# Partial sums of weight tiles made by DMA in DRAM, and nine more groups of seven products

## The chip, the cores and the metric

One core of one Trainium2 chip runs the whole program. The metric is the device time of one execution in microseconds; the median of several executions is compared. TensorE is called PE in the profile, VectorE DVE, ScalarE ACT, GpSimd POOL and SyncE SP.

## The reference

One decoder layer on 256 tokens of width 2048, in float32:

```python
u = rmsnorm(h, norm_mix_pre)
z, xbc, dt_raw, q, k, v = split(u @ w_in)          # w_in: 2048 x 12320
xbc = silu(causal_depthwise_conv(xbc, conv_w, conv_b))
y_ssm = rmsnorm_grouped(ssd_chunked(...) * silu(z)) # Mamba-2 scan, 32 heads
y_att = dilated window attention of q, k, v         # 16 heads
h = h + rmsnorm(concat(y_ssm, y_att) @ w_out, norm_mix_post)          # w_out: 4096 x 2048
hdn = relu(rmsnorm(h, norm_mlp_pre) @ w_up)                           # w_up: 2048 x 8192
h = h + rmsnorm((hdn * hdn) @ w_down, norm_mlp_post)                  # w_down: 8192 x 2048
```

Nearly all of the work is the four weight matrices, 269 MB in float32, each multiplied once by 256 tokens.

## The kernel before

**Precision by splitting.** Every float32 factor is split into a rounded part hi and the rest lo, and a product is three matmuls: hi·hi, hi·lo and lo·hi (lines 262 to 264). A weight tile is 256 rows by 512 columns, laid out as 128 partitions x 2 x 512 (`raw`, 512 KB). `fetch` (line 144) loads it on SP's queue, ScalarE writes hi (line 139), VectorE lo = raw − hi (line 140). There are four `raw` buffers (`RAWS`) and five pairs of hi and lo (`BUFS`); a load waits until VectorE has read the last tenant of its buffer, and ScalarE waits until TensorE has used the hi buffer's last tenant. In some stages three more places for raw tiles lie in `uc`.

**Groups of seven.** `unit` (line 362) works two neighbouring column blocks of 512 at once, over all rows of K in steps of 256. For one such step there are, per column block, a 2 x 2 block of weights (two row tiles) and a 2 x 2 block of activations (two K tiles by two halves of the tokens). The plain way (`row_tiles`) takes eight products of three matmuls, 24. `seven` (line 311) does a Strassen-Winograd step instead: seven products, 21 matmuls. It needs four sums of activations, made once per set of activations and kept (`sums_of_acts`, line 293, in the places listed in `room["sums"]`), and four sums of weight tiles, made by VectorE each time. With a0, a1 and b0, b1 the two row tiles of the two column blocks, it makes e0 = a0 + b0, e1 = e0 + b1, t4 = e1 + a1 and, in place, b0 + b1, by four adds of 128x512 (`add_in_line`, line 223), and then splits a (two tiles), e (two), the b pair and t4 (one). `combine_new` and `combine_onto` bring the seven accumulators together at the unit's last group.

Which steps go by seven is written out: `V_SEVENS` (1, 3, 5, 6) for the V columns of w_in (two units of eight steps), lists in the calls of `unit` for w_out and w_down, and `UP_SEVENS` (2, 4, 5) for w_up. Of the eight w_up double blocks, the first is done in another way, so seven units by `unit` remain: three in the first half of the hidden width, four in the second. After each half its part of w_down follows: two units of 16 steps.

**Order.** The steps of `weights` and `seven` are given priority over the rest (`AHEAD`) and are kept in order among themselves by `in_line`. Side work, such as the turning of the last block's outputs, waits in a queue (`waiting`) and one piece of it is started after each step by `pump`. `mix_to_up` is an order written out by hand that covers the norm between w_out and w_up. Pool does a few small sums in the SSD part and the power −1/2 of the norms (lines 134, 885 and 1160); after the SSD part these are all that it does.

**Memory.** Pools are stacks: `cp` holds constants for the whole program, `mp` and `ap` the middle part, and `hp`, opened after `mid.close()`, the second part. `in_place_of_h` lends the room of `h` (`ha`, `hb`) to the sums of activations while h waits in DRAM (`h_d`).

Of the kernel before, what the change touches and what calls it, by code (L numbers as in the profile page):

```python
# [10 lines left out]
F32 = mybir.dt.float32  # L11
# [5 lines left out]
P = 128  # L17
# [22 lines left out]
KB = 2  # L40
MASKED = -1.0e30
# [10 lines left out]
UP_SEVENS = (2, 4, 5)  # L52
V_SEVENS = (1, 3, 5, 6)

# [20 lines left out]
def hymba_layer(ctx: ExitStack, tc: tile.TileContext, x, norm_mix_pre, w_in, conv_w, conv_b, dt_bias, a_log,  # L75
# [38 lines left out]
    cst = cp.tile([P, consts.shape[1]], F32, name="cst")  # L114
    ident = cst[:, 0:P]
    triu = cst[:, P:2 * P]
    two = cst[:, 2 * P:2 * P + 32]
    m0 = cst[:, 2 * P + 32:3 * P + 32]
    m1 = cst[:, 3 * P + 32:5 * P + 32]
# [23 lines left out]

    def fetch(src, k0, c0, step=KB, into=None):

        raw = wp.tile([P, KB, NB], F32, name="raw", bufs=RAWS) if into is None else into
        for j in range(0, KB, step):
            rs = slice((k0 + j) * P, (k0 + j + step) * P)
            nc.sync.dma_start(raw[:, j:j + step], src[rs, c0:c0 + NB].rearrange("(k p) n -> p k n", p=P))
        return raw  # L150
# [23 lines left out]
    def in_place_of_h(acts):  # L174

        a = hp.tile([P, 3 * KB, 2, S], F32R, name="ha")
        room["sums"] = [a[:, k] for k in range(3 * KB)]
        if acts is part:
            b = hp.tile([P, KB, 2, S], F32R, name="hb")
            room["sums"] += [b[:, k] for k in range(KB)]  # L180
            room["sums"] += [hp.tile([P, 2, S], F32R, name="wpost", bufs=2) for _ in range(2)]
        else:
            b = hp.tile([P, NT, NB], F32, name="hb")
            room["shared"] = [[b[:, t] for t in range(NT)],
                              [hp.tile([P, NB], F32, name="wpost", bufs=2) for _ in range(NT)]]
        room["raw"] = None
        room["acts"] = acts
        sums_of.clear()

    def fetch_next(src, k0, c0):  # L190

        if room["raw"] is None:
            return fetch(src, k0, c0)
        turn = room["turn"]
        room["turn"] += 1
        n = KB * (turn % (RAWS + (NK - SUMS) // KB - 1) - RAWS)
        return fetch(src, k0, c0, into=None if turn < 0 or n < 0 else room["raw"][:, n:n + KB])
# [25 lines left out]
    def add_in_line(dst, a, b):  # L223
        with in_line():
            line["dve"] = nc.vector.tensor_tensor(dst, a, b, op=ALU.add)  # L225
# [85 lines left out]
    def seven(src, ca, cb, k, acc, more, first, last):  # L311
# [4 lines left out]
        with tc.high_priority(offset=AHEAD):  # L316
            raw_a = fetch_next(src, k * KB, ca)
            raw_b = fetch_next(src, k * KB, cb)
            e, t4 = sum_tile(), tmp()
            add_in_line(e[:, 0], raw_a[:, 0], raw_b[:, 0])  # L320
            add_in_line(e[:, 1], e[:, 0], raw_b[:, 1])
# [3 lines left out]
            add_in_line(raw_b[:, 0], raw_b[:, 0], raw_b[:, 1])  # L325
# [33 lines left out]
    def order_of(ks, by_seven):  # L359
        return [(k, k in by_seven) for k in ks]  # L360
# [66 lines left out]
    cw = cp.tile([P, 4, 32], F32, name="cw")  # L427
    bias_b = cp.tile([P, 32], F32, name="bias_b")
    a_b = cp.tile([P, 32], F32, name="a_b")
    skip_b = cp.tile([P, 32], F32, name="skip_b")  # L430
# [19 lines left out]
    def load_parameters():  # L450
# [4 lines left out]
        nc.sync.dma_start(cst[:, P:], consts[:, P:])  # L455
# [77 lines left out]
    with tc.high_priority(offset=2 * AHEAD), tc.manual_schedule():  # L533
        nc.sync.dma_start(cst[:, 0:P], consts[:, 0:P])
# [21 lines left out]
    rbq = cp.tile([P, S], F32, name="rbq")  # L556

    mid = ExitStack()
# [5 lines left out]
    dt = cp.tile([P, NT, 32], F32, name="dt")  # L564
    dA = cp.tile([P, NT, 32], F32, name="dA")
    acs = cp.tile([P, NT, 32], F32, name="acs")
    eacs = cp.tile([P, 32], F32, name="eacs")
    toend = cp.tile([P, 32], F32, name="toend")
# [250 lines left out]
    def two_values(vb):  # L819
# [16 lines left out]
        unit(w_in[:, COL_V:], vb, order_of(range(7), V_SEVENS), (7,), acc, more,  # L836
# [15 lines left out]
    waiting.append(in_place_of_last_heads())  # L852
    qk.append(keys_too(1))
# [225 lines left out]
    early = 5  # L1079
    for k in range(early):  # L1080
# [16 lines left out]

    new_h()
# [19 lines left out]
    unit(w_out, 0, order_of(range(early, 14), (6, 9, 12)), (14, 15), acc, more,  # L1118
# [25 lines left out]
    unit(w_out, 2, order_of((0, 6, 1, 9, 2, 12, 3, 4, 5, 8, 7, 10), (6, 9, 12, 4, 8, 10)), (11, 13, 14, 15), acc, more,  # L1144
# [91 lines left out]
    for hf in range(2):  # L1236
        if hf:
            in_place_of_h(act_u)
        for fb in range(0 if hf else 2, 8, 2):
            unit(w_up[:, hf * 4096:], fb, order_of(range(6), UP_SEVENS), (6, 7), acc, more,  # L1240
                 lambda x: combine_new(room["shared"], x), 0, (up_end(fb, 0), up_end(fb + 1, 1)))
            acc, more = more, acc
        if hf == 0:
            in_place_of_h(part)
            unit(w_down, 0, order_of(range(14), (4, 6, 9, 11, 13)), (14, 15), acc, more,
                 lambda x: combine_new(in_mw(0), x), 0, (onto(0), onto(1)))
            unit(w_down, 2, order_of((0, 1, 4, 2, 6, 3, 9, 5, 11, 7, 13, 8), (4, 6, 9, 11, 13)), (10, 12, 14, 15), more, acc,
# [17 lines left out]
    unit(w_down[4096:], 0, order_of(range(14), (3, 6, 8, 11, 13)), (14, 15), acc, more,  # L1265
# [4 lines left out]
    unit(w_down[4096:], 2, order_of((0, 1, 3, 2, 6, 4, 8, 5, 11, 7, 13, 9), (3, 6, 8, 11, 13, 9)), (10, 12, 14, 15), more, acc,  # L1270
# [24 lines left out]
```

## Time and profile before

| | |
|---|---|
| median of 3 runs | 1473.71 us (1473.21 to 1474.2) |
| profiled execution: first to last instruction (span) | 1471.1 us |
| what the median has beside that span | 2.6 us |
| PE, DVE, ACT, POOL busy | 1461.2, 1239.6, 861.1, 47.8 us |
| granted clock of TensorE | 0.998 |
| moved by DMA | 287.31 MB, 195 GB/s on average |

The program's runs are timed without the profiler; the profiled execution has no other time of its own than its span, so the two are set against each other by the 2.6 us. Busy time of an engine is the union of its instructions' rows, so rows that overlap (an instruction starts before the one ahead of it has ended) count once. In a table of stages each row is a stretch in us from the start, its length, then for each engine the busy us and the count of instructions, the granted clock, the share of time that the 16 DMA engines are busy on average, and the rate in GB/s. In a list of DMA issues the last number is the median from issue to landing.

### The profile page before, as it was taken

What the parts mean: (1) busy time and instruction counts of PE and PEld (TensorE: products, weight loads), DVE (VectorE), ACT (ScalarE), POOL (GpSimd) and SP (SyncE); (2) the same over time, 40 slices, a digit from 0 to 9 for tenths busy, and PEclk for the clock granted to TensorE, in tenths of its full rate; (3) what the DMA queues carried; (4) which work ended last, traced back from release to release, by engine and by line L of the source; (5) the groups of instructions that cost most, each with busy time, mean ns of one, the idle gap of its engine ahead of it and who ended that gap; (6) DMA issues with size and microseconds to landing.
All of it is one profiled execution on the core that took longest, in us unless ns stands there. A gap on an engine that the chain in (4) does not pass through costs nothing.

```text
span 1471.1 us, 20006 instructions
## 1 busy us (share of the span) xinstructions
PE 1461.2 (99%) x7216; PEld 1231.4 (84%) x7216; DVE 1239.6 (84%) x1849; ACT 861.1 (59%) x1188; POOL 47.8 (3%) x67
## 2 busy tenths in 40 slices
PE   9999999999999999999999999999999999999998
PEld 8888888888888888888888888888888888888886
DVE  6798797898497696588989989889887898989998
ACT  7475675465456565555557566655554666665553
POOL 0003100210000000000000000000000000000000
PEclk9999999999999999999999999999999999999999
DMA  7665566555657476566657566655665666576853
GB/s 272 208 205 182 179 184 194 174 172 167 177 168 207 122 208 192 191 229 210 204 177 237 165 194 201 210 175 191 213 223 174 201 201 205 172 235 202 273 200 114
DMA packets 151299, 287.31 MB, mean 195 GB/s; under 512 B 11696, under 2 KB 14624, under 8 KB 151200
## 3 DMA queue, kind: packets, MB, share of 16 engines
q1 hardware_dynamic: 143472, 272.50, 58.9%
q10 hardware_dynamic: 7728, 13.54, 2.8%
q8 instruction: 56, 0.92, 0.3%
q14 instruction: 43, 0.35, 0.1%
HBM read 281.78 MB, written 4.23 MB: 194 GB/s over the span
## 4 chain that ended last, share of the span: by engine, by line
PE 94%; DVE 3%; issue 1%; ACT 1%; DMA 1%; POOL 0%; POOLq 0%; SPq 0%; ACTq 0%; DVEq 0%
PE acc L393 17%; PE acc L262 12%; PE acc L263 12%; PE acc L264 12%; PE acc L396 9%; PE acc L345 4%; PE acc L346 4%; PE acc L344 4%; PE ps L263 3%; PE ps L262 3%; PE ps L264 3%; PE ps L346 2%; PE ps L344 2%; PE ps L345 2%; DVE lo L140 1%
## 5 line engine op out<-in xcount | busy, mean ns | idle before, releaser
L139 ACT ACTIVATE hi<-raw 128x1024 fp32r<-128x1024 f32 (+1 forms) x477 | 499.0, 1053 | 387.9 <-PE acc L393 111.9
L140 DVE TENSOR_TENSOR lo<-raw,hi 128x1024 fp32r<-128x1024 f32 (+1 forms) x477 | 579.9, 1220 | 135.7 <-ACT hi L139 127.9
L393 PE MATMUL acc<-ua,hi 128*128 128x512 f32 x680 | 186.3, 402 | 0.0
L393 PEld LDWEIGHTS acc<-ua,hi 128*128 128x128 f32 x680 | 119.7, 189 | 18.7
L262 PE MATMUL acc<-hi,ua 128*128 128x512 f32 x280 | 112.0, 400 | 0.0
L396 PEld LDWEIGHTS acc<-ua,lo 128*128 128x128 f32 x680 | 99.8, 189 | 11.6
L264 PE MATMUL acc<-hi,ua 128*128 128x512 f32 x280 | 109.3, 391 | 0.0
L263 PE MATMUL acc<-lo,ua 128*128 128x512 f32 x280 | 109.3, 390 | 0.0
L396 PE MATMUL acc<-ua,lo 128*128 128x256 f32 x680 | 102.9, 281 | 0.0
L262 PE MATMUL acc<-hi,sh 128*128 128x512 f32 x224 | 88.7, 397 | 0.0
L264 PE MATMUL acc<-hi,sl 128*128 128x512 f32 x224 | 87.3, 390 | 0.0
L263 PE MATMUL acc<-lo,sh 128*128 128x512 f32 x224 | 87.3, 390 | 0.0
L139 ACT ACTIVATE hi<-e 128x1024 fp32r<-128x1024 f32 x51 | 54.1, 1062 | 55.5 <-DVE e L225 50.3
L393 PE MATMUL acc<-uc,hi 128*128 128x512 f32 x272 | 77.6, 398 | 0.0
L263 PE MATMUL acc<-lo,ah 128*128 128x512 f32 x168 | 65.5, 390 | 0.4 <-DVE lo L140 0.4
L264 PE MATMUL acc<-hi,al 128*128 128x512 f32 x168 | 65.4, 389 | 0.0
L262 PE MATMUL acc<-hi,ah 128*128 128x512 f32 x168 | 65.4, 389 | 0.0
L264 PEld LDWEIGHTS acc<-hi,ua 128*128 128x128 f32 x280 | 52.6, 188 | 11.6
L140 DVE TENSOR_TENSOR lo<-e,hi 128x1024 fp32r<-128x1024 f32 x51 | 62.0, 1216 | 0.0
L262 PEld LDWEIGHTS acc<-hi,ua 128*128 128x128 f32 x280 | 52.6, 188 | 10.4 <-ACT ua L141 0.3
L263 PEld LDWEIGHTS acc<-lo,ua 128*128 128x128 f32 x280 | 52.7, 188 | 10.0
L264 PE MATMUL acc<-hi,uc 128*128 128x512 f32 x144 | 56.0, 389 | 0.0
(475 smaller groups left out, 3060.9 us busy)
## 6 DMA issues: line engine op xcount, KB each, us to landing
raw<-in_w_in_dram SPq DMA_DIRECT2D x189, 512.0 KB, 3.6
raw<-in_w_up_dram SPq DMA_DIRECT2D x128, 512.0 KB, 3.9
raw<-in_w_down_dram SPq DMA_DIRECT2D x110, 512.0 KB, 4.7
raw<-in_w_out_dram SPq DMA_DIRECT2D x46, 512.0 KB, 4.2
uc<-in_w_out_dram SPq DMA_DIRECT2D x18, 512.0 KB, 4.5
uc<-in_w_down_dram SPq DMA_DIRECT2D x18, 512.0 KB, 5.1
bc<-acs_d ACTq DMA_DIRECT2D x8, 512.0 KB, 4.5
xs<-in_x_dram SPq DMA_DIRECT2D x8, 256.0 KB, 6.3
```

What stands on the lines that cost most here:

```text
L139: return (nc.scalar.activation(hi, src, AF.Copy), nc.vector.tensor_tensor(lo, src, hi.bitcast(F32), op=ALU.subtract))
L140: nc.vector.tensor_tensor(lo, src, hi.bitcast(F32), op=ALU.subtract))
L262: nc.tensor.matmul(dst, a_h[:, r, ts], hi[:, j], start=begin and j == 0, stop=False)
L263: nc.tensor.matmul(dst, a_h[:, r, ts], lo[:, j], start=False, stop=False)
L264: product[t] = nc.tensor.matmul(dst, a_l[:, r, ts], hi[:, j], start=False, stop=end and j == KB - 1)
L344: nc.tensor.matmul(dst, a_h, hi[:, j], start=own and first, stop=False)
L345: nc.tensor.matmul(dst, a_h, lo[:, j], start=False, stop=False)
L346: nc.tensor.matmul(dst, a_l, hi[:, j], start=False, stop=own and last)
L393: nc.tensor.matmul(acc[f], hi[:, j, f * P:(f + 1) * P], u(k0 + j), start=k0 + j == 0, stop=False, skip_group_check=True)
L396: nc.tensor.matmul(acc[f][:, 0], lo[:, j, f * P:(f + 1) * P], u(k0 + j)[:, 0], start=False, stop=k0 + j == NK - 1, skip_group_check=True)
```

## The change

- **Sums in DRAM.** For every group of seven, b0 + b1 is made by DMA: Pool's queue copies b0 (256 KB) from the weights to one of five places in DRAM, and then copies b1 onto it with an add. `plan` lists all groups in order ahead of time, and `next_pair` issues the two transfers for the next one on the list. Four are issued ahead, behind the last heads of the SSD part; each group then asks for the one four groups later. The first use of a place is preceded by a small transfer from `sh`, which makes Pool wait until the SSD part has written it.
- **The group.** The b tile is loaded in two issues of 256 KB: the sum b0 + b1 from its place into `raw_b[:, 0]`, and b1 from the weights. VectorE makes e1 = a0 + (b0 + b1), e0 = e1 − b1 and t4 = e1 + a1: three adds instead of four.
- **Constants.** What only the first half reads (`triu`, `two`, the masks, the convolution's weights, `dt` and its like) moves from `cp` to a pool `fp` that `mid.close()` closes; `ident` becomes a tile of its own. In that room `hp` gets `hc`, a place for one more set of sums of activations.
- **More groups.** `UP_SEVENS` becomes (1, 2, 4, 5), and in both units of the first w_down half step 2 joins (4, 6, 9, 11, 13). That is 68 groups instead of 59. The order of the steps in the second of these units changes with it.

```diff
+PAIRS_AHEAD = 4
-UP_SEVENS = (2, 4, 5)
+UP_SEVENS = (1, 2, 4, 5)
...
+    mid = ExitStack()
+    fp = mid.enter_context(tc.tile_pool(name="fp", bufs=1))
+    ident = cp.tile([P, P], F32, name="ident")
+    cst = fp.tile([P, consts.shape[1] - P], F32, name="cst")
...
-    def fetch(src, k0, c0, step=KB, into=None):
+    def fetch(src, k0, c0, step=KB, into=None, pair=None):
         raw = wp.tile([P, KB, NB], F32, name="raw", bufs=RAWS) if into is None else into
+        if pair is not None:
+            nc.sync.dma_start(raw[:, 0], pair)
+            nc.sync.dma_start(raw[:, 1], src[(k0 + 1) * P:(k0 + 2) * P, c0:c0 + NB])
+            return raw
...
-        room["sums"] = [a[:, k] for k in range(3 * KB)]
+        room["sums"] = [a[:, k] for k in range(3 * KB)] + [hc[:, k] for k in range(KB)]
...
+    def next_pair():
+
+        if not pairs:
+            return
+        src, ca, k = pairs.pop(0)
+        cb = slice(ca + NB, ca + 2 * NB)
+        d = places[len(paired) % len(places)]
+        if len(paired) < len(places):
+            nc.gpsimd.dma_start(d[:, 0:1], sh[:, NK - 1, 0:1].bitcast(F32))
+        nc.gpsimd.dma_start(d, src[k * KB * P:(k * KB + 1) * P, cb])
+        nc.gpsimd.dma_start(d, src[(k * KB + 1) * P:(k * KB + 2) * P, cb], accum_op=ALU.add)
+        paired.append((src, ca, k, d))
+
+    paired = []
+    places = [dram.tile([P, NB], F32, name=f"pair{i}") for i in range(PAIRS_AHEAD + 1)]
+
+    def pair_of(src, ca, k):
+
+        next_pair()
+        s_, c_, k_, d = paired[turn_of["pair"]]
+        assert (s_ is src) and (c_, k_) == (ca, k), (c_, k_, ca, k)
+        turn_of["pair"] += 1
+        return d
...
             raw_a = fetch_next(src, k * KB, ca)
-            raw_b = fetch_next(src, k * KB, cb)
+            raw_b = fetch_next(src, k * KB, cb, pair_of(src, ca, k))
             e, t4 = sum_tile(), tmp()
-            add_in_line(e[:, 0], raw_a[:, 0], raw_b[:, 0])
-            add_in_line(e[:, 1], e[:, 0], raw_b[:, 1])
+            add_in_line(e[:, 1], raw_a[:, 0], raw_b[:, 0])
+            add_in_line(e[:, 0], e[:, 1], raw_b[:, 1], ALU.subtract)
             hl_a = parts()
             split_in_line(*hl_a, raw_a)
             add_in_line(t4, e[:, 1], raw_a[:, 1])
-            add_in_line(raw_b[:, 0], raw_b[:, 0], raw_b[:, 1])
...
+            plan(("down", 0), w_down, 0, range(14), (2, 4, 6, 9, 11, 13))
+            plan(("down", 0), w_down, 2, (0, 2, 1, 4, 3, 6, 5, 9, 7, 11, 8, 13), (2, 4, 6, 9, 11, 13))
...
+    with tc.high_priority(offset=AHEAD):
+        for _ in range(PAIRS_AHEAD):
+            next_pair()
     qk.append(keys_too(1))
...
+    hc = hp.tile([P, KB, 2, S], F32R, name="hc")
+    hp.tile([P, S], F32, name="edge_h")
     new_h()
```

More of the change, by code (lines that the diff above doesn't have):

```diff
@@ L834, in end @@
             return at_end
-        unit(w_in[:, COL_V:], vb, order_of(range(7), V_SEVENS), (7,), acc, more,
+        unit(w_v, vb, orders["v", vb], (7,), acc, more,
              lambda x: combine_new([[v[:, t] for t in range(NT)] for v in values], x), 0, (end(0), end(1)))
@@ L1078, in hymba_layer @@
     acc = [bank() for _ in range(2 * NT)]
-    early = 5
-    for k in range(early):
+    for k in range(EARLY):
         for b in range(2):
@@ L1116, in whole @@
         return at_end
-    unit(w_out, 0, order_of(range(early, 14), (6, 9, 12)), (14, 15), acc, more,
+    unit(w_out, 0, orders["out", 0], (14, 15), acc, more,
          lambda x: combine_new(in_mw(0), x), 0, (whole(0), whole(1)), first=False)
@@ L1239, in hymba_layer @@
         for fb in range(0 if hf else 2, 8, 2):
-            unit(w_up[:, hf * 4096:], fb, order_of(range(6), UP_SEVENS), (6, 7), acc, more,
+            unit(w_ups[hf], fb, orders[("up", hf), fb], (6, 7), acc, more,
                  lambda x: combine_new(room["shared"], x), 0, (up_end(fb, 0), up_end(fb + 1, 1)))
```

77 lines of the change are left out of this document (46 added, 31 removed).

## The prediction

> **What bounds the kernel now.** I read the page's engine line and chain first, then the table of stages, then one group of seven instruction by instruction, and last the transfers.
>
> ```profile
> span 1471.1 us, 20006 instructions
> PE 1461.2 (99%) x7216; PEld 1231.4 (84%) x7216; DVE 1239.6 (84%) x1849; ACT 861.1 (59%) x1188; POOL 47.8 (3%) x67
> PE 94%; DVE 3%; issue 1%; ACT 1%; DMA 1%; POOL 0%; POOLq 0%; SPq 0%; ACTq 0%; DVEq 0%
> ```
>
> TensorE is busy over 99% of the span and carries 94% of the chain that ended last, so only fewer matmuls, or new holes between them, move the time. VectorE at 84% is second. That is an average; what matters is how close it comes to the length of each stage.
>
> ```profile
> core 0: us, PE busy (x) PEld busy (x) DVE busy (x) ACT busy (x) POOL busy (x), PEclk, DMA share, GB/s
> 409.00:449.00 40.00, 39.73 (x180) 32.65 (x179) 37.23 (x45) 23.37 (x27) 0.00 (x0) 1.00 0.66 195
> 628.00:689.00 61.00, 61.00 (x271) 50.53 (x271) 53.27 (x71) 33.22 (x40) 0.00 (x0) 1.00 0.71 237
> 866.00:909.70 43.70, 43.70 (x201) 36.11 (x200) 38.70 (x47) 28.40 (x36) 0.00 (x0) 1.00 0.64 196
> 952.70:1041.00 88.30, 88.30 (x396) 73.05 (x395) 77.78 (x102) 48.44 (x56) 0.00 (x0) 1.00 0.60 197
> 1041.00:1110.00 69.00, 69.00 (x306) 57.11 (x306) 60.02 (x70) 37.72 (x40) 0.00 (x0) 1.00 0.63 213
> 1295.10:1386.40 91.30, 91.30 (x410) 75.54 (x409) 86.25 (x114) 51.52 (x62) 0.00 (x0) 1.00 0.70 234
> 1386.40:1452.00 65.60, 65.19 (x288) 53.63 (x287) 61.61 (x76) 37.93 (x43) 0.00 (x0) 1.00 0.55 186
> ```
>
> In order: the first V unit, the end of the first W_out unit, one W_up unit (seven of these run), the two units of the first W_down half, the two of the second. Columns after the first are busy time with the count. A W_up unit leaves VectorE 43.70 − 38.70 = 5.0 us idle. Where VectorE fills 93 or 94% of the stretch TensorE loses a little: 0.27 us in the V unit, 0.41 us in the last one. At 94.5% (1295 to 1386, with fewer groups of seven per us) it loses nothing.
>
> **TensorE: 27 matmuls fewer.** A pair of K tiles for two column blocks costs 24 matmuls, as a group of seven 21. Groups now: V 8, W_out 9, W_up 7 × 3 = 21, W_down 21, together 59. After: W_up 7 × 4 = 28, first W_down half 12, the rest as before: 68. Nine more groups remove 27 matmuls of 128x512. The duration in a matmul's own row is about 390 ns, but they overlap, so the price is their spacing. Between 1041 and 1110 nearly all work is such matmuls and nothing is idle: 69.00 / 306 = 0.2255 us. 27 × 0.2255 = **6.1 us**, all on the bounding path: seven units lose 3 × 0.2255 = 0.68 us each, two more lose the same.
>
> **VectorE.** One group of seven, in order of time:
>
> ```profile
> start us, us, engine line op out<-in xcount [idle before <-releaser]
> 880.85 0.68 DVE L225 TENSOR_TENSOR e<-raw 128x512 f32<-128x512 f32 x1
> 881.57 0.69 DVE L225 TENSOR_TENSOR e<-e,raw 128x512 f32<-128x512 f32 x1
> 882.18 1.22 DVE L140 TENSOR_TENSOR lo<-raw,hi 128x1024 fp32r<-128x1024 f32 x1
> 883.31 0.69 DVE L225 TENSOR_TENSOR r<-e,raw 128x512 f32<-128x512 f32 x1
> 883.92 0.69 DVE L225 TENSOR_TENSOR raw<-raw 128x512 f32<-128x512 f32 x1
> 884.52 1.22 DVE L140 TENSOR_TENSOR lo<-e,hi 128x1024 fp32r<-128x1024 f32 x1
> 885.87 1.23 DVE L140 TENSOR_TENSOR lo<-raw,hi 128x1024 fp32r<-128x1024 f32 x1
> 887.01 0.68 DVE L140 TENSOR_TENSOR lo<-r,hi 128x512 fp32r<-128x512 f32 x1
> 887.61 0.68 DVE L225 TENSOR_TENSOR e<-raw 128x512 f32<-128x512 f32 x1
> ```
>
> Again the spacing is the cost. The `raw<-raw` add is the sum b0 + b1 that the change takes from DRAM instead: 884.52 − 883.92 = 0.60 us less in each of the 59 groups, 35 us over the kernel. The whole group takes 887.61 − 880.85 = 6.76 us, afterwards 6.16. A pair done the plain way has two 1024 splits of 883.31 − 882.18 = 1.13 us, 2.26. So a pair turned into a group adds 3.9 us of VectorE. A W_up unit goes from 38.70 to 38.70 − 3 × 0.60 + 3.9 = 40.8 us, while TensorE shrinks it to 43.70 − 0.68 = 43.0: 95% full, idle 2.2 us instead of 5.0. The first W_down half's first unit goes to 77.78 − 5 × 0.60 + 3.9 = 78.7 of 87.6, which still has room. V, W_out and the second W_down half only get lighter.
>
> One more set of activation sums is made three times (twice for W_up, once for W_down), each one add of 512, three smaller ones and a split:
>
> ```profile
> L302 DVE TENSOR_TENSOR r<-ah,al 128x512 f32<-128x512 f32 x11 | 7.5, 684 | 0.0
> L303 DVE TENSOR_TENSOR r<-r 128x256 f32<-128x256 f32 x23 | 9.7, 422 | 1.4 <-PE acc L1223 0.7 <-PE ps L1141 0.2
> L304 DVE TENSOR_TENSOR r<-r 128x128 f32<-128x128 f32 x23 | 6.7, 289 | 0.5
> L305 DVE TENSOR_TENSOR r<-r 128x128 f32<-128x128 f32 x23 | 6.6, 287 | 0.4
> ```
>
> That is 0.68 + 0.42 + 2 × 0.29 + 0.68 = 2.4 us at most, 7 us in all, beside TensorE; the W_down one lands in the unit above (81.1 of 87.6). I cost it at nothing; with the cover gone it is up to 7 us.
>
> I take what a VectorE that is 95% full costs TensorE from the two stretches at 93 and 94%: 0.3 us a unit, 7 × 0.3 = **2.1 us lost**. Those two stretches get 4 and 6 adds lighter, so their 0.27 and 0.41 us should go: **0.7 us gained**.
>
> **Transfers.** Per group the change adds on Pool's queue a copy of 256 KB from DRAM to DRAM and an accumulating copy of 256 KB onto it; the SP queue then reads that sum in place of b0, so what SP moves stays the same, in one more instruction (0.37 us, below). No run shows an accumulating transfer or one issued by Pool.
>
> ```profile
> q1 hardware_dynamic: 143472, 272.50, 58.9%
> 880.96 0.37 SPq L149 DMA_DIRECT2D raw<-in_w_up_dram  x1
> raw<-in_w_up_dram SPq DMA_DIRECT2D x16, 512.0 KB, 4.3
> q10 hardware_dynamic: 956, 2.86, 14.6%
> raw<-in_w_out_dram SPq DMA_DIRECT2D x16, 512.0 KB, 5.6
> raw<-in_w_down_dram SPq DMA_DIRECT2D x24, 512.0 KB, 4.9
> h_d<-ha ACTq DMA_DIRECT2D x6, 256.0 KB, 4.3
> ha<-h_d ACTq DMA_DIRECT2D x6, 256.0 KB, 6.9
> ```
>
> Row 1: 0.589 × 16 × 1471.1 / 143472 = 0.097 us per 2 KB packet. 256 KB is 128 rows, 8 packets on each of 16 engines, 0.77 us. I price the copy at 0.77 and the accumulate between 0.77 (one pass) and 1.54 (source and sum both read), and take 0.77, as every packet in the trace has that price. Four groups a W_up unit: 6.2 to 9.2 us of the 16 engines on top of 0.64 × 43.7 = 28, so the share rises from 0.64 to 0.79, or 0.87.
>
> What that does to the loads is read from stretches with a second queue at work. In the W_up unit a load lands 4.3 us after its issue; at share 0.71, beside the second queue's 14.6%, 5.6; at 0.70 in the second W_down half, 4.9. The two loaded stretches (61.00 of 61.00, 91.30 of 91.30) cost TensorE nothing. The slack: the load issued at 880.96 holds the second matrix of the group that VectorE starts at 887.61; landing at 885.3 it is 2.3 us early. After the change the group ahead is 0.60 shorter and the tile takes two issues (0.37), so 1.4 us are left: a landing up to 5.7 us is free. I expect 5 to 5.7 and charge nothing.
>
> The Trainium skill speaks against the change here: "Collectives: The Full Stack", section "The bandwidth ceiling: the fold count and why AG ≠ RS ≠ AR", says that an add made in the transfer reads two sources, and so runs at about half a copy's rate. By it the accumulate takes 1.54 us; no run here shows it yet.
>
> Pool waits for the copy before it issues the accumulate, and for the read of the place's last tenant. Behind these on Pool stand only the square roots of the later norms, issued after the last group ahead of them, and nobody needs them sooner. The moved constants are the same transfers into other tiles; I cost them at nothing, covered by the first weight tiles' work.
>
> **Sum.** −6.1 + 2.1 − 0.7 = −4.7 us on the profiled span, 1471.1 to 1466.4. The median of the runs, 1473.71, lies 2.6 us above that span and I keep this offset: **1469.0 us**. A measurement of this kernel can tell about 0.2%, 2.9 us, from no change; faster means below 1470.8, slower above 1476.7.
>
> **Rivals.**
>
> *Late loads (slower).* The place: the load of the b tile ahead of each of a W_up unit's four groups. A load that meets the copy and a doubled accumulate lands at 4.3 + 0.77 + 1.54 = 6.6 us instead of 4.3; starting from the 4.9 of W_down, 7.2. I price the middle, 6.9: 1.2 us past the free 5.7, four times a unit, 4.8, of which 2.2 idle VectorE time covers part: 2.6 × 7 = 18 us, less the 6.8 saved: **about 1485 us**. Milder, at 6.5, it is 1.0 × 7 = 7, no gain. It turns to a loss when landing passes 6.5 us. For it: the share of 0.87 is above anything in the trace. Against it: idle transfer time between bursts, and loaded stretches that cost nothing.
>
> *VectorE sets the W_up units (no change).* The units stay at 43.7 because 95% cannot be scheduled without holes; the gain is only W_down's 2 × 0.68 and the 0.7: 1473.7 − 2.1 = **1471.6 us**. For: 39.73 of 40.00 at 93%. Against: nothing lost at 94.5%.
>
> *The sums come late, so the change does not do what it says (slower).* SP would wait for a sum with all later loads behind it. A pair takes copy plus accumulate; by the last two rows 4.3 to 6.9 us each, 8.6 to 13.8. A W_up unit asks for one every 43.0 / 4 = 10.8 us, four ahead. At 13.8, with no overlap between pairs, a unit takes 55 us: 7 × 12 = 84 us more, **1551 us**. Against: the next copy can start while an accumulate is in flight.
>
> **How the numbers follow.** Forecast 0.56 (1466.9 to 1470.7: the holes between 0 and 0.55 us a unit), VectorE-bound 0.12, late loads 0.28, late sums 0.04. Faster 0.56, within 0.2% 0.12, slower 0.32. The range runs from 1466.4, no holes at all with the gaps gone (1473.7 − 6.8) less the 0.5 by which the runs shown differ from their median, to 1482, which takes in the milder two thirds of the late-load case; the rest and the late sums are left out. The forecast's own range is 1466.9 to 1470.7.
>
> **What would show it.** Matmuls 7189; 68 rows of three adds instead of 59 of four; VectorE near 40.8 us in a W_up unit, and its length 43.0 to 43.5 us. Landings of `w_up` loads at 5 to 5.7 us confirm the transfer step; above 6.5, with ScalarE or VectorE waiting for `raw` ahead of groups and holes between matmuls, the late-load rival holds. SP waiting on Pool's transfers would show late sums. The prediction is wrong if W_up units are longer than 43.7 us.

## The result, and the profile after

The changed kernel takes 1494.51 us (median; 1492.58 to 1496.69) against 1473.46 us for the kernel before on the same chip: ratio 1.0143, 95% interval 1.0131 to 1.0155. It is 21 us slower, where 4.7 us faster was forecast. The profiled execution, whose span is 1494.9 us, is the longest of the four, 2.2 us above their median. Its page, as far as it answers to the lines shown of before:

```profile
span 1494.9 us, 20376 instructions
PE 1466.0 (98%) x7189; PEld 1224.8 (82%) x7189; DVE 1240.7 (83%) x1850; ACT 871.4 (58%) x1209; POOL 143.5 (10%) x208
q1 hardware_dynamic: 144560, 272.50, 58.3%
q0 software_dynamic: 15392, 35.66, 11.9%
PE 64%; DVE 16%; DMA 12%; ACT 4%; issue 3%; POOL 0%; SPq 0%; POOLq 0%; DVEq 0%; ACTq 0%
```

The 27 matmuls are gone (7216 to 7189), and the engines' busy times have hardly moved. What moved is the chain: TensorE carried 94% of it and carries 64% now; VectorE has 16% and DMA, which had 1%, 12%. Pool's queue q0 is new, 11.9% of all sixteen engines' time. No single engine became the bound; the chain passes through transfers and VectorE's work instead.

`unit` works seven double blocks of w_up, W_up units 1 to 7. Here are 2, 3, 5, 6 and 7 (1 and 4 follow another stage), in the columns of the table of stages; the W_up row shown of before was unit 2, 43.70 us with all 43.70 busy, and the others were 43.0 to 44.3 us long:

```profile
871.80:916.40 44.60, 43.44 (x198) 35.22 (x197) 40.41 (x50) 29.21 (x39) 5.44 (x8) 1.00 0.82 231
916.40:964.10 47.70, 45.44 (x207) 36.51 (x206) 40.27 (x49) 30.15 (x40) 4.89 (x7) 1.00 0.79 229
1180.70:1225.50 44.80, 44.78 (x205) 36.74 (x204) 40.08 (x49) 29.24 (x38) 5.45 (x8) 1.00 0.84 236
1225.50:1273.30 47.80, 44.10 (x197) 34.86 (x197) 40.48 (x50) 29.68 (x39) 5.45 (x8) 1.00 0.81 225
1273.30:1320.70 47.40, 44.67 (x205) 35.97 (x204) 40.21 (x48) 30.15 (x39) 4.89 (x7) 1.00 0.80 226
```

VectorE has 40.1 to 40.5 us, near the forecast 40.8, and the DMA share is 0.79 to 0.84. Two units are nearly as long as before, three are 3 to 5 us longer, at the same share and the same work. So what costs the time is not in the sums of these columns; the traces below look for it in which instruction meets which transfer.

The loss by stage, worked out from the records: by how much the stage is longer than before, and behind L what TensorE lost there, the sum over neighbouring matmul starts of what they are apart beyond 0.227 us (counted from 0.06 us on). The last columns are kernels from the experiments below.

```
us            after         no transfers  acc. alone    acc. behind    order 0,3,1..
                            (a_src)       (a_acc)       small copy     (a_0312)
V1           +0.7  L 7.7   -2.1  L 6.1   -2.3  L 6.0   +0.0  L 6.2   -1.0  L 6.2
V2           +2.7  L 3.4   +0.9  L 2.2   +1.3  L 2.2   +0.4  L 3.2   +2.4  L 3.0
W_out        -0.5  L 2.6   +0.7  L 2.6   +0.3  L 2.6   +0.7  L 2.6   -0.4  L 2.6
W_up 1       +2.8  L 5.8   +2.0  L 5.3   +2.4  L 5.5   +2.5  L 5.5   +0.0  L 4.7
W_up 2-3     +5.7  L 5.3   +1.1  L 2.3   +1.3  L 2.8   +5.1  L 4.8   +3.7  L 1.1
W_down, up 4 +5.9  L10.6   +0.0  L 2.0   -0.5  L 2.1   +3.6  L 7.7   +3.5  L 8.8
W_up 5-7     +8.3  L 9.3   -2.3  L 1.9   +0.5  L 3.6   +4.8  L 6.7   +1.0  L 1.8
W_down 2     -2.8  L 0.4   -1.2  L 0.3   -1.6  L 0.3   -2.5  L 0.8   -2.9  L 0.4
the end      +1.0  L 3.2   +1.2  L 3.2   +1.0  L 3.2   +1.3  L 3.2   +1.1  L 3.2
all          L 48.2        L 25.9        L 28.2        L 40.6        L 31.8
```

The kernel before has L 21.0 in all; by stage, in the same order, 6.8, 2.2, 2.6, 2.7, 0.7, 0.8, 1.1, 1.0 and 3.2. (What the changed kernel loses more in V1 it loses in the first 108 us, ahead of Pool's first transfer.) The changed kernel lost 27 us more between its matmuls, which turned the 6 us of fewer matmuls into a loss. Two kinds of hole stand out; how the 27 us divide between them and others is not worked out.

**Late loads.** The chain of waits at the end of W_up unit 6, then Pool's and TensorE's instructions of the same moment:

```profile
1259.12 8.59 DMA raw<-in_w_up_dram
1267.70 0.02 issue
...
1267.81 1.06 ACT hi L143
1268.87 0.61 ACT junk L1270
1269.48 0.61 ACT r L1270
...
1270.52 0.62 ACT r L1271
```

```profile
1256.93 0.81 POOL L258 DMA_DIRECT2D pair<-in_w_down_dram  x1 [6.52 <-DMA pair<-in_w_down_dram]
1268.38 0.39 PE L311 MATMUL acc<-hi,uc 128*128 128x512 f32 x1
1270.66 0.55 PE L1282 MATMUL ps<-ident,junk 128*128 128x128 f32 x3 [1.90 <-ACT junk L1271]
```

Line 258 is the accumulate. It is issued at 1256.93 and, by its record, lands at 1265.73. Three loads of weights are issued behind it, at 1257.24, 1259.12 and 1261.45, and land at 1266.37, 1267.70 and 1268.97, one behind the other and all behind it: 7.5 to 9.1 us, where 4 are usual. ScalarE stands at the split of the first for 5.4 us, and behind that split in its queue wait the scalings of unit 6's own first outputs (`junk` and `r`, lines 1270 and 1271). TensorE needs those for its transposes and starts them 2.3 us after the last matmul. The engines' waits over the whole run point the same way; the first two lines are of the kernel before, the others of the changed one:

```profile
ACT hi L139 <- DMA raw<-in_w_up_dram: 23.9, 23, 1.6
ACT hi L139 <- DMA raw<-in_w_down_dram: 20.2, 17, 3.1
```

```profile
ACT hi L143 <- DMA raw<-in_w_up_dram: 37.7, 31, 5.4
ACT hi L143 <- DMA raw<-in_w_down_dram: 35.6, 26, 4.9
DVE e L233 <- DMA raw<-pair: 19.7, 14, 3.9
POOL pair L257 <- DMA raw<-pair: 542.1, 44, 74.6
```

(Us in total, times, longest.) The last line says that Pool mostly waits for a place to be read: the sums are not late. That an engine other than TensorE waits costs nothing in itself; the chain above shows one place where it did.

**A bank handed over.** The start of the same unit:

```profile
1230.82 1.22 DVE L144 TENSOR_TENSOR lo<-e,hi 128x1024 fp32r<-128x1024 f32 x1
...
1231.96 1.22 DVE L144 TENSOR_TENSOR lo<-raw,hi 128x1024 fp32r<-128x1024 f32 x1
...
1233.09 0.68 DVE L144 TENSOR_TENSOR lo<-r,hi 128x512 fp32r<-128x512 f32 x1
1233.69 1.28 DVE L144 TENSOR_TENSOR sl<-acc,sh 128x512 fp32r<-128x512 f32 x2
1234.43 0.19 PEld L390 LDWEIGHTS acc<-hi,ha 128*128 128x128 f32 x1 [2.04 <-DVE sl L144]
```

With step 1 a group of seven, the products of the unit's second step want the `acc` banks in which the last unit's outputs still stand, turned and waiting to be split (`sl<-acc`). These splits stand in VectorE's queue behind three splits of the group itself. TensorE's weight load waits 2.0 us for them, a wait that no row of before has: there step 1 was plain. Over the whole run TensorE idles 5.3 us for such splits, in four places:

```profile
PE acc L390 <- DVE sl L144: 2.7, 2, 1.6
PE acc L390 <- DVE al L144: 2.6, 2, 1.5
```

### The profile page after: what moved, and what is told of

Its sections match the earlier page's. It is cut to its first block, busy times and chain, and to the rows that moved or that the text cites. A ratio compares the mean times of both kernels' runs of the same rounds, so it can differ in the third digit from the quotient of the medians.

```text
span 1494.9 us, 20376 instructions
## 1 busy us (share of the span) xinstructions
PE 1466.0 (98%) x7189; PEld 1224.8 (82%) x7189; DVE 1240.7 (83%) x1850; ACT 871.4 (58%) x1209; POOL 143.5 (10%) x208
## 3 DMA queue, kind: packets, MB, share of 16 engines
q0 software_dynamic: 15392, 35.66, 11.9%
## 4 chain that ended last, share of the span: by engine, by line
PE 64%; DVE 16%; DMA 12%; ACT 4%; issue 3%; POOL 0%; SPq 0%; POOLq 0%; DVEq 0%; ACTq 0%
PE acc L449 17%; DVE lo L144 10%; PE acc L452 8%; PE acc L309 7%; PE acc L311 7%; PE acc L310 7%; DMA raw<-pair 4%; DMA raw<-in_w_down_dram 4%; DMA raw<-in_w_up_dram 3%; DVE e L233 3%; ACT hi L143 2%; PE acc L392 2%; PE acc L390 2%; PE acc L391 2%; PE ps L310 1%
## 5 line engine op out<-in xcount | busy, mean ns | idle before, releaser
L143 ACT ACTIVATE hi<-e 128x1024 fp32r<-128x1024 f32 x60 | 63.7, 1061 | 114.3 <-DVE e L233 105.8
L309 PE MATMUL acc<-hi,ua 128*128 128x512 f32 x236 | 94.0, 398 | 0.0
L310 PE MATMUL acc<-lo,ua 128*128 128x512 f32 x236 | 92.2, 391 | 0.0
L311 PE MATMUL acc<-hi,ua 128*128 128x512 f32 x236 | 92.1, 390 | 0.0
L309 PE MATMUL acc<-hi,sh 128*128 128x512 f32 x212 | 84.0, 397 | 0.0
L311 PE MATMUL acc<-hi,sl 128*128 128x512 f32 x212 | 82.6, 390 | 0.0
L310 PE MATMUL acc<-lo,sh 128*128 128x512 f32 x212 | 82.6, 390 | 0.0
L144 DVE TENSOR_TENSOR lo<-e,hi 128x1024 fp32r<-128x1024 f32 x60 | 73.1, 1218 | 0.0
L309 PE MATMUL acc<-hi,uc 128*128 128x512 f32 x144 | 56.0, 390 | 1.5 <-ACT hi L143 1.5
L233 DVE TENSOR_TENSOR e<-raw 128x512 f32<-128x512 f32 x55 | 37.8, 687 | 23.1 <-DMA raw<-pair 19.7
L310 PE MATMUL acc<-lo,uc 128*128 128x512 f32 x144 | 56.0, 389 | 0.0
L311 PE MATMUL acc<-hi,uc 128*128 128x512 f32 x144 | 56.0, 389 | 0.0
```

The source lines that it names most:

```text
L143: return (nc.scalar.activation(hi, src, AF.Copy), nc.vector.tensor_tensor(lo, src, hi.bitcast(F32), op=ALU.subtract))
L144: nc.vector.tensor_tensor(lo, src, hi.bitcast(F32), op=ALU.subtract))
L233: line["dve"] = nc.vector.tensor_tensor(dst, a, b, op=op)
L309: nc.tensor.matmul(dst, a_h[:, r, ts], hi[:, j], start=begin and j == 0, stop=False)
L310: nc.tensor.matmul(dst, a_h[:, r, ts], lo[:, j], start=False, stop=False)
L311: product[t] = nc.tensor.matmul(dst, a_l[:, r, ts], hi[:, j], start=False, stop=end and j == KB - 1)
```

## The experiments

Three theories stood at first. The bank handover (A in the expectations); the transfers, whose landings come late (the prediction's first rival); and a VectorE that is too full. Each kernel's time is set against runs of the kernel before on the same chip.

### Undoing one part

```diff
 a_src, in the kernel after: no transfers by Pool, b0 is loaded in place of the sum
-            nc.sync.dma_start(raw[:, 0], pair)
+            nc.sync.dma_start(raw[:, 0], src[k0 * P:(k0 + 1) * P, c0:c0 + NB])
 a_0312: another order of W_up's steps;  a_0312_src: both
-                plan(("up", hf), w_ups[hf], n, range(6), UP_SEVENS)
+                plan(("up", hf), w_ups[hf], n, (0, 3, 1, 2, 4, 5), UP_SEVENS)
 a_59, in the kernel after: the old 59 groups (UP_SEVENS (2, 4, 5), old W_down lists)
 b145, in the kernel before: UP_SEVENS = (1, 4, 5)
```

> The changed kernel without Pool's transfers: the place of b0 + b1 is loaded with b0 itself from the weights, in the same two issues (so the sums are left out and the output is not the layer's). Groups, order and VectorE's work are those of the changed kernel. A: the handover stays, 1480 to 1486. B: the loss goes, 1467 to 1470. C: 1494.5.

1473.15 us, ratio 0.9996 (0.9987 to 1.0005): all 21 us are back, as theory B has it, but not the gain that it expected on top.

> The changed kernel with W_up's steps in the order 0, 3, 1, 2, 4, 5: the same 68 groups and the same transfers, but the first group stands at the third place again and four stand in a row. A: 10 to 14 us of the loss comes back, 1480 to 1484. B: 1494.5 within 3, the transfers are the same. C: four in a row are worse for VectorE, 1494.5 or more.

1484.76 us, 1.0074 (1.0055 to 1.0093): 10 us are back, with all transfers and all groups in place, just short of what theory A expected.

> The changed kernel with W_up's steps in the order 0, 3, 1, 2, 4, 5 and without Pool's transfers (b0 itself loaded in the sum's place, so the sums are left out and the output is not the layer's). Handover and transfers as two separate causes: both gone, 1467 to 1469, the 6.1 us of matmuls earned. If four groups in a row fill VectorE even with three adds: 1473 or more.

1473.33 us, 1.0000 (0.9990 to 1.0009): with no transfers the order is worth nothing.

> The kernel before with one edit: W_up's three groups of seven stand at steps 1, 4, 5 instead of 2, 4, 5. Same matmuls, same VectorE work, no transfer by Pool. Theory A (bank handover: a unit's first group of seven writes into the four banks from which the last unit's outputs are still being turned; at step 1 it does so one step earlier): W_up units 1.5 to 2 us longer, seven of them, 1484 to 1488 us. Theory B (Pool's transfers make the loads land late): 1473.5 within 2. Theory C (VectorE is full): 1473.5 within 2.

1478.45 us, 1.0036 (1.0023 to 1.0049): a group on step 1 costs the kernel before 5 us, less than half of what theory A expected, and more than the other two did.

> The changed kernel with the 59 groups of before: sums in DRAM, three adds, but W_up at 2, 4, 5 and the first W_down half without step 2. A: 1471 to 1474, first group at the third place and VectorE lighter. B: nine pairs of transfers fewer of 68 and 6 us of matmuls more: 1485 to 1495. C: VectorE lighter than before, 1473 or less.

1475.36 us, 1.0013 (1.0004 to 1.0023): sums in DRAM for the old groups cost 2 us and gain none, though VectorE's busy time falls from 1239.6 to 1207.0 us. Theory B, which expected 1485 to 1495 from the transfers alone, missed.

What follows: the loss needs Pool's transfers, and added groups beside them; with the old groups the transfers cost 2 us, and without the transfers the new groups cost nothing. With no transfers the order of W_up's steps is worth nothing (a_src against a_0312_src), with all of them 10 us. That is more than the handover itself: TensorE's idle time for `sl` and `al` is 5.3 us in the changed kernel, 1.2 in a_src, 1.1 in b145 and none in a_0312. The order also moves the loads against the transfers, and no run parts the two. Even with neither in the way nine groups and 27 matmuls fewer bring nothing: the holes grow from 21.0 to 25.9 us in a_src, and eat 4.9 of the 6.1.

### Which of the two transfers

```diff
 a_copy: the accumulate left out;  a_2copy: a plain copy in its place
-        nc.gpsimd.dma_start(d, src[(k * KB + 1) * P:(k * KB + 2) * P, cb], accum_op=ALU.add)
 a_acc: the copy left out after the first five
-        nc.gpsimd.dma_start(d, src[k * KB * P:(k * KB + 1) * P, cb])
+        if len(paired) < len(places):
+            nc.gpsimd.dma_start(d, src[k * KB * P:(k * KB + 1) * P, cb])
 a_half: groups 2 and 5 of each W_up unit load b0 themselves
```

> The changed kernel with the accumulating transfer left out: Pool issues the copy of b0 alone (the sums are not made, the output is not the layer's). Leaving out all of Pool's transfers gave back 21.4 us. If an accumulate reads two sources and takes two thirds of the pair's time on the DMA engines: 1480. If both weigh the same: 1484. If the copy from DRAM to DRAM is the dearer: 1487 or more.

1475.93 us, 1.0010 (1.0000 to 1.0019).

> The changed kernel with the copy left out behind the first five: Pool issues the accumulate alone, onto what the place held (the sums are wrong, the output is not the layer's). Accumulate two thirds: 1487. Both the same: 1484. Copy the dearer: 1480 or less. Pool's chain per pair is also halved, as in the run with the copy alone, so that by itself it does not tell the two apart.

1475.13 us, 1.0013 (1.0003 to 1.0022). Each transfer alone costs 2 to 3 us, so they fit no division of the 21 us: their costs do not add up to that of the pair.

> The changed kernel with a second plain copy in place of the accumulate (the place ends as b1, the sums are left out, the output is not the layer's). A copy alone takes the DMA engines 4.1% of 1474 us / 68 = 0.9 us, an accumulate alone 8.3%, 1.8 us. Two copies are 1.8 us, the load of the run with the accumulate alone, but two transfers one after the other as in the changed kernel. If the share of DMA time decides: 1475 to 1478. If it is that two transfers in sequence lie beside twice as many loads: 1485 to 1495.

1479.42 us, 1.0039 (1.0025 to 1.0053), between the two forecasts.

> The changed kernel in which W_up's groups 2 and 5 load b0 itself instead of a sum from DRAM (their sums are left out, the output is not the layer's): two pairs of transfers a W_up unit instead of four. All four: 1494.5, none at all anywhere: 1473.2. If the loss goes with the number of pairs: 1484. If there is a threshold in the DMA share between 0.77 and 0.81: 1475 to 1478.

1483.95 us, 1.0066 (1.0041 to 1.0091), over a wide range, 1478.50 to 1491.32. That is the figure expected if the loss goes with the number of pairs, but the stages tell otherwise. Little is left in W_up's units 5 to 7 (−1.3 us against before, where the changed kernel had +8.3); the first W_down half with the unit after it is now 8.5 us longer, where it had 5.9, though the transfers there are the same.

Pool's queue in a_copy and then in a_acc, packets, MB and share of sixteen engines:

```profile
q0 software_dynamic: 5600, 17.83, 4.1%
```

```profile
q0 software_dynamic: 10352, 19.14, 8.3%
```

0.041 × 1474.2 / 68 = 0.89 us of all engines for a copy; (0.083 × 1473.5 − 5 × 0.89) / 68 = 1.73 us for an accumulate, 1.95 times as much. This is the rule that the prediction cites from the Trainium skill, "Collectives: The Full Stack", section "The bandwidth ceiling: the fold count and why AG ≠ RS ≠ AR" (an add made in the transfer runs at about half a copy's rate; stated there of reductions between cores), and the trace agrees with the factor. The prediction took 0.77 for both.

Either transfer alone costs 2 to 3 us, two plain copies 5 to 6, a copy and an accumulate 21. Either the share passes some point between 0.78 and 0.82, or it matters when the accumulate is issued: alone, right when a place has been read; behind a copy, when that has landed, some 5 us later.

### The share, or the moment

```diff
 a_acc_late: each sum's copy (after the first five) cut to one column; the accumulate waits for it
+            nc.gpsimd.dma_start(d[:, 0:1], src[k * KB * P:(k * KB + 1) * P, cb][:, 0:1])
 a_phase: one place more; the accumulate is issued behind the NEXT sum's copy
 a_early: one place more; hold Pool until the last sum is read, then the older accumulate, then the copy
+                nc.gpsimd.tensor_copy(mark, turn_of["raw"][:, 0, 0:1])
+            add_pair()
 a_par: the accumulate goes to other places, which nobody reads
```

> The kernel after, where the copy of each sum after the first five is cut to one number a row (the sums are then not the reference's); the accumulate waits for that small copy as it waits for the whole one in the kernel after, so it falls 2 us or more behind the moment the place was read, with nearly the traffic of the kernel that left the copy out (1475.1). Share theory: 1475 to 1477. Phase theory: back toward the loss, 1480 to 1495.

1487.56 us, 1.0096 (1.0079 to 1.0114), as the phase theory has it. The W_up unit 6 in a_acc, in this kernel, and in a_0312:

```profile
1208.50:1252.50 44.00, 43.72 (x200) 35.66 (x199) 40.31 (x49) 29.35 (x38) 3.25 (x4) 1.00 0.78 211
```

```profile
1219.30:1265.30 46.00, 43.97 (x200) 35.34 (x199) 40.44 (x49) 29.68 (x39) 5.43 (x8) 1.00 0.78 209
```

```profile
1216.30:1260.70 44.40, 44.40 (x205) 36.14 (x204) 40.43 (x49) 29.74 (x38) 5.44 (x8) 1.00 0.82 236
```

The DMA share of the first two is the same 0.78, and the second is 2 us longer; the third has the highest share, 0.82, and is short. Over the kernel the small copies (3.9 us from issue to landing) add 12 us, though between 355 us and the end of the W_up units the mean share is 0.73 in both. The second W_down half of the changed kernel runs at a higher share yet, and loses nothing:

```profile
1320.70:1409.00 88.30, 88.30 (x395) 72.74 (x394) 81.43 (x106) 50.74 (x62) 8.17 (x12) 1.00 0.85 267
```

And Pool's queue has 4.2% of the engines in c_down (below), which loses 9.7 us, and 10.5% in a_59, which loses 2:

```profile
q0 software_dynamic: 5312, 12.06, 4.2%
q0 software_dynamic: 13376, 30.94, 10.5%
```

So the share does not decide. The loads of the five W_up units, sorted by whether an accumulate was in flight when they were issued, and how long it had been (count, median us to landing, landings over 6.5 us):

```
             none in flight     issued 0 to 2.5 us ago   longer ago
after         57  4.22   0       13  7.93  10             29  4.34   4
a_acc         76  4.41   2       10  5.45   3             13  4.52   0
a_acc_late    52  4.01   0       18  6.72  11             29  4.71   4
a_0312        52  4.25   1       20  5.36   5             28  4.90   1
a_src         99  4.03   0       -                        -
```

In the changed kernel 10 of the 14 late loads are among the 13 issued within 2.5 us behind an accumulate, and none is among the 57 that met none. In all of that kernel 60 loads are issued so, with a median of 6.55 us and 31 over 6.5; 57 loads of a_copy stand so behind a plain copy, with 5.09 and 6. But that is not the whole account. From 355 us on the changed kernel has 38 more loads over 6.5 us, 18 of them with no accumulate in flight; the kernel before has 14 there, and no transfer by Pool. And a_acc, which loses 2 us in all, has 53 loads within 2.5 us behind an accumulate, a median of 6.38 and 25 over 6.5. A late load is not by itself a loss; which of them cost TensorE time, these counts don't tell.

> The kernel after, with the same 68 copies and 68 accumulates and the same groups; Pool issues the accumulate of a sum one turn later, right behind the next sum's copy, so both leave the moment a place has been read, instead of the accumulate some 4 to 5 us later when its own copy has landed (one more place, so that every sum is still ready as early as before). Share theory (the loss is what the transfers' share of the DMA engines costs): unchanged, 1490 to 1497. Phase theory (the loss comes because the accumulate falls on the next group's loads, which then land only with it): 1475 to 1481.

1491.16 us, 1.0124 (1.0107 to 1.0141).

> The kernel after, with all its copies and accumulates and the same groups, where Pool is now held by a tiny copy of one column of the buffer that the last sum was read into, and then issues the accumulate of the sum copied one turn earlier and, half a microsecond later, the next copy. (In the run that only put the accumulate behind the next copy, it still waited for that copy to land, and left 4.2 us behind the read as before: that run moved nothing.) Share theory: unchanged, 1488 to 1495. Phase theory (loads issued within 2.5 us behind an accumulate are the ones that land late, and the accumulate's moment decides which): 1474 to 1482, with most of the late loads of W_up's units gone.

1493.57 us, 1.0137 (1.0122 to 1.0153). Neither moved the accumulates. Pool in a_early, where w_in's groups end and w_out's begin (line 271 is the accumulate, 257 the hold, 261 the copy):

```profile
419.97 0.81 POOL L271 DMA_DIRECT2D pair<-in_w_in_dram  x1 [4.20 <-DMA pair<-in_w_in_dram]
427.83 0.73 POOL L257 COPY edge_l<-raw 128x1 f32<-128x1 f32 x1 [7.05 <-DMA raw<-pair]
428.51 0.54 POOL L261 DMA_DIRECT2D pair<-in_w_out_dram  x1
432.69 0.81 POOL L271 DMA_DIRECT2D pair<-in_w_out_dram  x1 [3.65 <-DMA pair<-in_w_out_dram]
```

As the kernel is written, the accumulate of w_in's last sum would stand between the hold and the copy of w_out's first. It does not: it left at 419.97, and the accumulate at 432.69 reads w_out, so it belongs to the copy at 428.51 just ahead of it. Pool's queue has the instructions in another order than the text of the kernel. In a_phase, a_early and the three versions with their edits below, the n-th accumulate waits for the landing of the n-th copy, its own, as in the changed kernel, and leaves 0.3 us behind it. So the remark in the expectation of a_early, that the accumulate waits for the next sum's copy, is wrong; and these kernels repeat the changed kernel with one more place (a_early with the hold besides) rather than test the moment.

> The changed kernel with the accumulate sent to another place, so that it need not wait for the copy (the sums are wrong, the output is not the layer's). Same DMA time, 2.6 us a pair, in about half the stretch. If the share of DMA time decides: 1490 to 1497. If the length of the stretch does: 1478 to 1485.

1565.49 us, 1.0618 (1.0602 to 1.0635), and this tells nothing on the question: as nobody reads these places, nothing held the accumulates back, and they all left in the first 139 us.

```profile
0.00:130.00 130.00, 70.32 (x300) 59.17 (x301) 32.70 (x50) 34.51 (x62) 54.54 (x72) 0.75 1.06 230
```

The engines are full (1.06), the first loads starve, and TensorE has 70 of 130 us busy; 88.8 us are lost before the first V unit's end, and the rest runs like a_copy.

### Other versions

```diff
 b_d6: no transfers, four adds on VectorE, UP_SEVENS (2, 4, 5), step 2 joins in the first W_down half
 c_down: sums in DRAM for W_down's 23 groups alone, 61 groups
 c_down_phase, c_down_early, a_0312_phase: with the edits of a_phase or a_early
```

> A candidate: the changed kernel's rooms and its two more groups in the first W_down half, W_up at 2, 4, 5, and all sums by VectorE's four adds as before, no transfer by Pool: 61 groups. 2 x 0.68 = 1.4 us of matmuls fewer where VectorE has room (77.8 of 88.3 us, plus 4.5 and the sums): 1472.1. If the room is not enough there, 1473.5 or more.

1476.99 us, 1.0023 (1.0013 to 1.0032): without the transfers, with four adds, two groups more in W_down lose about 3.5 us.

> A candidate: sums in DRAM for the 23 groups of W_down alone, two of them new; W_in, W_out and W_up as before with VectorE's four adds, W_up at 2, 4, 5. 61 groups, 6 matmuls fewer. If W_down has room on the DMA engines (share 0.60 to 0.70 before): 1471 to 1473. If 23 pairs of transfers cost what they earn: 1473.4 or more.

1483.89 us, 1.0066 (1.0051 to 1.0081), far past both forecasts: the second unit of the first W_down half is 10.9 us longer. Its chain, and Pool's issues:

```profile
1048.51 5.84 DMA raw<-pair
...
1060.33 7.96 DMA raw<-in_w_down_dram
...
1073.11 6.71 DMA raw<-pair
```

```profile
1047.09 0.82 POOL L258 DMA_DIRECT2D pair<-in_w_down_dram  x1 [4.96 <-DMA pair<-in_w_down_dram]
1054.64 0.54 POOL L257 DMA_DIRECT2D pair<-in_w_down_dram  x1 [6.74 <-DMA raw<-pair]
1058.95 0.82 POOL L258 DMA_DIRECT2D pair<-in_w_down_dram  x1 [3.76 <-DMA pair<-in_w_down_dram]
1067.66 0.54 POOL L257 DMA_DIRECT2D pair<-in_w_down_dram  x1 [7.90 <-DMA raw<-pair]
```

Here the two sides lock. A read of a sum lands, 0.3 us later the copy leaves, lands in 4 us and lets the accumulate go; 1 to 2 us behind it SP issues the next group's two loads, which land just behind the accumulate, 5 to 8 us later; that landing frees the next place, and so on, every 11 to 13 us, six accumulates running (1047 to 1107 us). This kernel has 23 accumulates where a_59 has 59, and two groups more; it loses 9.7 us where a_59 loses 2.

> The kernel with sums in DRAM only for W_down's groups (61 groups of seven; 1483.9 as it stood, with 10.9 us lost in one unit where the loads landed with the accumulates), with the accumulate one turn later. Share theory: 1482 to 1486. Phase theory: the unit gives back most of its 10.9 us, 1473 to 1477, which would be the best version with sums in DRAM and may equal the kernel before.

1479.77 us, 1.0041 (1.0026 to 1.0056), some 3 us less than c_down, each against the kernel before on its chip; all that it has over c_down in fact is a sixth place.

> Sums in DRAM for W_down's groups alone (61 groups of seven), with the accumulate held and issued as in the run beside it. Share theory: as that version stood, 1480 to 1484. Phase theory: the two units of the first W_down half gain instead of losing, as they did where no accumulate was in their way (7 us shorter than before there), and the whole comes out at 1466 to 1474, below the kernel before.

1486.18 us, 1.0086 (1.0069 to 1.0103).

> The kernel after with W_up's order 0, 3, 1, 2, 4, 5 (no group of seven on a unit's second step) and the accumulates one turn later as in the run beside it. Share theory: as the order alone, 1483 to 1487. Phase theory: 1472 to 1477, some 10 us under the order alone; no gain over the kernel before is expected, since the same order without any of Pool's transfers stood at 1473.3.

1485.74 us, 1.0080 (1.0065 to 1.0095): as a_0312 without it. These three moved no accumulate either, so they say nothing on the phase theory.

No version beat the kernel before; a_src and a_0312_src equal it, and these leave the sums out.

**What is settled and what is not.** Shown: the loss comes with Pool's transfers and added groups together; the share of the DMA engines does not set it; most of the late loads in the five W_up units stand right behind accumulates; the order of W_up's steps is worth 10 us with the transfers and nothing without. Open: whether the whole traffic with the accumulates at another moment would be free, since no run moved them; which of the late loads cost time; how the 10 us divide between the handover and the loads; and why a load waits for an accumulate issued before it by another engine. (The DMA engines did not stand idle meanwhile: between 1260 and 1263 us, in the late loads shown, they were busy 0.90 and moved 173 GB/s, where between 1254 and 1257 it was 1.01 and 328 GB/s.) a_acc_late speaks for the moment, but its small copies are traffic of their own kind, if little of it: the 75 loads of its run that met only a small copy had a median of 4.29 us.

## Why the prediction was wrong

- **Matmuls.** 27 fewer, as counted, and the spacing held. It was wrong that all 6.1 us lie on the bounding path: without any transfers 4.9 of them go into holes (a_src).
- **VectorE.** 40.8 us forecast for a W_up unit, 40.1 to 40.5 measured. The holes, 0.3 us a unit, are 0.5 in units 2, 3, 5, 6 and 7 of a_src (4.2 us there against 1.8 before, over five), inside the forecast's own range; the first unit lost 2.6 us more than before. The V unit, one of the stretches from which the 0.3 came, has a group on step 1 too, but no unit of this kind runs just ahead of it; the W_up units run back to back.
- **Handover.** The step that is missing: costing a group by its engine time, the prediction did not ask which bank the unit's second step writes, and what stands ahead in VectorE's queue of the split that frees it. Measured, TensorE's idle time for that split is 5.3 us in the changed kernel and none in a_0312, with another order. The order as a whole is worth 10 us there, and 5 in the kernel before (b145, where only 1.1 us is that wait); the rest of these is not traced.
- **The gaps.** 0.7 us in V and the second W_down half. Right: the V unit's is gone in the changed kernel (no stall in the same 40 us), and the second W_down half's L fell from 1.0 to 0.4.
- **Transfers, the step that decided.** The share was right, 0.79 to 0.84 against 0.79 or 0.87. The transfers were charged nothing, and with the added groups they cost 21 us (a_src gives all of it back). The accumulate was taken at 0.77 us and is 1.73, above the upper bound of 1.54. And "a landing up to 5.7 us is free, I expect 5 to 5.7" was worked out for a median. The median of `w_up` loads came out lower than that, 4.5 us, but 14 of the 99 loads in five units took more than 6.5 us. The bound was held against an average share, though a load does not meet an average: it meets an accumulate just ahead of it (median 7.93 us in these units) or none (4.22).
- **Pool.** That its waits harm nobody held for the sums' being in time (late sums, 1551 us, did not come). But its wait for the copy sets the moment of the accumulate. That this moment is the harm is what a_acc_late speaks for; it isn't shown beyond that.
- **The rivals.** Late loads, 0.28 and 1485 us, is the one that came, in sign and in kind, with its place half wrong: more of the waiting was at tiles' splits on ScalarE (37.7 and 35.6 us, of which 64.5 for plain steps' tiles; 23.9 and 20.2 before) than at a group's b tile (19.7 us at line 233), and in the chain that ended last the reads of sums have 4% of the span, the loads of w_down 4% and those of w_up 3%. Its "turns to a loss past 6.5 us" was a condition on every load; in the five units a seventh of them came so late. VectorE-bound units would have given 1471.6, with W_up units as long as before. Without the transfers they nearly are (217.2 us for the five in a_src, 218.4 before; 1473.15 in all); whether VectorE is the reason no run shows.

## What to carry to other kernels

When a change adds transfers, don't hold a mean share or a median landing against the slack: list which loads are issued right behind a new transfer, give them its whole time on top as a bad case, and look at what else stands in the queue behind the instruction that waits for them. When a unit's order changes, write down for its first steps which accumulators they reuse and what is queued ahead of the instruction that frees these. And price work taken from an engine that is not the bound at nothing until a run shows what it frees: 33 us less of VectorE, with the old groups, bought no time here (a_59). When an edit is meant to move an instruction, look in the trace whether it moved before reading anything from the time: five kernels here were written to issue the accumulates a turn later, and none did.

## What the runs showed of the hardware

- An accumulating transfer of 256 KB from DRAM to DRAM holds the engines 1.73 us, 1.95 times a copy's 0.89.
- The counter of HBM reads does not show a read of the place that is added to. Before and after:

```profile
HBM read 281.78 MB, written 4.23 MB: 194 GB/s over the span
HBM read 317.43 MB, written 39.88 MB: 239 GB/s over the span
```

  Both rose by 35.65 MB, 68 × 2 × 0.262; the old contents of the place are 17.8 MB more, and are in neither.
- An accumulate leaves 0.3 us behind the landing of its own copy (median of the changed kernel's 68), which lands a median of 4.8 us after its issue in a_copy; the next sum's copy can leave while the accumulate is in flight (in a_early one is in flight from 432.69 to 439.55 us, and the next copy leaves at 433.84).
- Loads on another engine's queue that are issued up to 2.5 us behind an accumulate land later: in the changed kernel after a median of 6.55 us, against 4.27 with none in flight. Behind a plain copy it is 5.09 against 4.05 (a_copy), less than half as much more.
